# The second product of an attention score: from 64 partitions to all 128

## The chip, the cores and the metric

The kernel runs on one core of a Trainium2 chip. Its engines work side by side and each takes its own instructions in order: PE (TensorE) multiplies matrices, and its weight loads stand in the trace under their own name, PEld; DVE (VectorE), ACT (ScalarE) and POOL (GpSimd) work on elements; SP (SyncE) issues DMAs. On-chip data has 128 partitions; a matrix product sums over the partitions of its two operands. The metric is the device time of one execution in microseconds (us).

## The reference

Four transformer layers over 256 tokens and 1024 columns, batch 1: two layers of a first block (an attention of 16 heads with a mask of mixed dilations, and a differential attention of 16 score maps) and two of a second block (a gated delta rule, a windowed attention of 16 query heads on 2 key heads, and a feed-forward part). What matters here are the scores, which all three attentions compute in the same way:

```python
sc = jnp.einsum('mbqhd,mbkhd->mbhqk', qblk, ks,
                preferred_element_type=jnp.float32) * (dh ** -0.5)
...
sc = jnp.where(kpos[None, :] <= qpos[:, None], sc, NEG)
p = jax.nn.softmax(sc, axis=-1)
a = p[0] - lam * p[1]
return jnp.einsum('bhqk,bkhe->bqhe', a, vf)
```

These lines are the differential attention's; the other two differ in the mask, in what is made of the probabilities and in the number of keys. `dh` is 64. There are 96 score maps of 256 by 256 tokens: 16 + 16 in each of the two layers of the first block, and 16 in each of the two layers of the second. Above the diagonal block a map is masked, so that three of its four blocks of 128 by 128 are used.

## The kernel before

**Products in two parts.** TensorE reads its operands in a rounded format. So each f32 operand is split into a rounded part and what the rounding leaves out ("hi" and "lo"). A weight product is three matrix products into one PSUM bank: hi by hi, hi by lo, lo by hi (lines 312 to 314 for 512 columns a piece, lines 353 to 355 for 256).

**Scores.** A head has 64 columns, and two heads stand on the 128 partitions. `into_stack` (lines 454 to 463) writes a head's queries onto all 128: the rounded queries on one half of the partitions, their remainder on the other half. `into_keys` (lines 465 to 483) writes the rounded keys `kh` onto one half (line 474), and SP copies them to the other half by DMA (`twin`, line 480, two DMAs for a group of eight heads). So one product over 128 partitions gives (rounded + remainder of q) by rounded k (line 492). What the rounded keys leave out, `kl`, stands on a head's own half alone (line 475), and the second product (line 493) takes 64 partitions of the queries and of `kl`. A score map takes two such pairs, four products of 256 columns into one bank `sc`: tokens of block 1 first, then block 0.

**Order of the work.** The weight products are the main line. Everything else is queued by hand at a step of it (`at`, `tick`, with a lag in steps); the engines then run the instructions in the order in which the program wrote them. For one group of eight heads the order is: product for q, product for k, product for v, then the scores and the rest of each head between the weight products that follow. A head is: scores on PE, masked sum and row maximum on DVE (line 497), exponentials on ACT, in the first block a product with the mask's counts on DVE, transposes on PE (line 504), a copy on ACT (line 506), the product with v on PE (lines 510 to 512).

**Weights.** SP loads pieces of 256 rows (line 274, three buffers `raw`), ACT rounds them (line 284, `hi`), DVE subtracts (line 285, `lo`), with four buffers each of `hi` and `lo`.

**Second block.** Its windowed attention has two key heads. Their keys are written twice beside each other before the transpose, so that `kTh` and `kTl` (lines 958 and 959) stand on both halves already.

The tile `kl` is one of a ring of two buffers with the tag "Y"; a group of heads takes one of them.

Of the kernel before, what the change touches and what calls it, by code (L numbers as in the profile page):

```python
# [12 lines left out]
F32 = mybir.dt.float32  # L13
# [3 lines left out]
ALU = mybir.AluOpType  # L17
# [14 lines left out]
def _tables():  # L32
    """Masks, the identity and rotary tables: shapes alone decide them."""
    p = np.arange(128)[:, None]
    f = np.arange(128)[None, :]
    parts = {}
    parts["ident"] = (p == f).astype(np.float32)

    def band(count):
        return np.concatenate([count(128 + p, f), count(128 + p, 128 + f), count(p, f)], 1)  # L40

    def mix(t, s):
        d = t - s
        near = ((d >= 0) & (d <= 128)).astype(np.float32)
        return near + ((d >= 0) & (d % 4 == 0)) + ((d >= 0) & (d % 16 == 0))

    ca = band(mix).astype(np.float32)
    parts["ca"] = ca
    parts["ba"] = np.where(ca > 0, 0.0, NEG)
    parts["bb"] = np.where(band(lambda t, s: (s <= t)), 0.0, NEG)  # L50
    parts["bs"] = np.where(band(lambda t, s: (s <= t) & (t - s < 128)), 0.0, NEG)
    upper = (p <= f).astype(np.float32)
    one = np.ones((128, 128), np.float32)
    parts["mi"] = np.concatenate([upper, one], 1)
    parts["ng"] = np.where(parts["mi"] > 0, 0.0, NEG)
    parts["b16"] = p // 16 == f // 16
    parts["nb16"] = -parts["b16"].astype(np.float32)
    half = np.arange(0, 16, 2, dtype=np.float32)
    inv = (1.0 / np.power(np.float32(THETA), half / np.float32(16))).astype(np.float32)
    ang = (np.arange(256, dtype=np.float32)[:, None] * inv[None, :]).astype(np.float32)  # L60
    c, s = np.cos(ang), np.sin(ang)
    cc = np.concatenate([c, c], 1).reshape(2, 128, 16).transpose(1, 0, 2).reshape(128, 32)
    ss = np.concatenate([-s, s], 1).reshape(2, 128, 16).transpose(1, 0, 2).reshape(128, 32)
    parts["cc"], parts["ss"] = cc, ss
    f2 = np.power(np.float32(THETA), -np.arange(8, dtype=np.float32) * np.float32(0.125))
    parts["if"] = np.broadcast_to(f2.astype(np.float32)[None, :], (128, 8))
    where, col = {}, 0
    for k, v in parts.items():
        where[k] = (col, v.shape[1])
        col += v.shape[1]  # L70
    return np.ascontiguousarray(np.concatenate(list(parts.values()), 1).astype(np.float32)), where
# [6 lines left out]
def body(ctx: ExitStack, tc: tile.TileContext, I, out, upto=None):  # L78
# [60 lines left out]
    def column_load(name):  # L139
        """A vector of the model's width, its 128-element pieces in the columns of vT."""  # L140
        n, c = int(np.prod(I[name].shape)) // 128, vcol[name]
        row = half_tile("row")[0:n, 0:128]
        nc.scalar.dma_start(row, rows(I[name], 0, n))

        def compute():
            p = wk([128, 512])
            T.transpose(p[:, 0:n], row, ident[0:n, 0:n])
            V.tensor_copy(vT[:, c:c + n], p[:, 0:n])
        return compute
# [4 lines left out]
    def lam_load():  # L154
        """The first block's lambda of each layer."""
# [36 lines left out]
    def trig():  # L192
        """Rotary tables of the second block, from the positions."""
# [94 lines left out]
    def feed():  # L288
        """Loads and splits ahead as far as the buffers released before the last step allow."""
# [26 lines left out]
    def proj(lh, evac, sweep=False):  # L316
        """[tokens, columns] of lh @ the next weights, one bank per token block; evac(bank, block)."""
# [26 lines left out]
    def proj_w(lh, evac):  # L344
        """[columns, tokens] of 512 columns: two banks of two 128-column chunks; evac(bank, index)."""
# [21 lines left out]
    def to_lh(lh, src, c0, t, scale=None):  # L367
        """Transposes the 512 columns of src [128 tokens of block t, 512] into chunks c0.. of lh, split."""
# [33 lines left out]
    def into_silu(dst, hr, gain=None):  # L402
        """(tanh(z/2) + 1) * z', z' before its norm factor: hr * dst is silu (hr None: a half of it)."""
# [14 lines left out]
    def rope(x, h, cc, ss):  # L418
        """x [128, h * 64] of one token block: turns the first 16 of every 64 columns, in place."""
# [15 lines left out]
    def turned(r, tabs, then, lag):  # L435
        """Scales, turns and transposes 8 heads, two of them on the partitions; then(bank, columns, block)."""
# [17 lines left out]
    def into_stack(dst, r, tabs):  # L454
        """Eight heads of queries into dst [128, 8, 256]: a head's rounded columns on one half of the partitions,
        the one of its place in its pair, and what they leave out on the other."""
# [8 lines left out]
    def into_keys(st, r, tabs):  # L465
        """Eight heads of keys: rounded ones on both halves of the partitions, what they leave out on their own."""
        def then(p, cols, t):
            if t == 0:
                st["kh"] = act.tile([128, 8, 256], F32R, name="kh", tag="LT", bufs=1)
                st["kl"] = act.tile([128, 4, 256], F32R, name="kl", tag="Y", bufs=2)  # L470
            for i in range(2):
# [3 lines left out]
                V.tensor_tensor(out=st["kl"][a, :, cols], in0=p[a], in1=h.bitcast(F32), op=ALU.subtract)  # L475
            if t == 1:
                def twin():
                    for i in range(2):
                        a, b = halves(i)
                        nc.sync.dma_start(st["kh"][b, i:8:2, :].bitcast(F32), st["kh"][a, i:8:2, :].bitcast(F32))  # L480
                at(0, twin)
# [4 lines left out]
    def scores(q, kh, kl, i, bias):  # L486
        """Masked scores of one head, [t1 x s0 | t1 x s1 | t0 x s0], and their row maxima; i is its place in its pair."""
        sc = wk([128, 512], "sc")
        half = slice(64 * i, 64 * i + 64)
        for o, t in ((0, 1), (256, 0)):  # L490
            c = slice(128 * t, 128 * t + 128)
            T.matmul(sc[:, o:o + 256], q[:, c], kh, start=True, stop=False)
            T.matmul(sc[:, o:o + 256], q[half, c], kl[half], start=False, stop=True)  # L493
# [26 lines left out]
    def gate_first(gate):  # L520
        """gate <- (gate + 1) * bank"""
# [4 lines left out]
    def gate_second(gate, m1, lm, g):  # L526
        """m1 + (gate + 1) * bank, halved, transposed and split into lm"""
# [13 lines left out]
    def rstd_root(dst, a, b, c=0.0):  # L541
        """dst <- (a + b + c)^-1/2"""
# [3 lines left out]
    def rstd(dst, a, b):  # L546
        """dst * ROOT = rsqrt((a + b) / DM + eps)"""
        rstd_root(dst, a, b, DM * 1e-6)

    def prepare(t, scale, groups=(0, 1), lag=1.2):  # L550
        """Column groups of token block t of X are ready: their transposes for the next products, and the norm factors."""
# [18 lines left out]
    def normed(t, r, scale, k, folded=None):  # L570
        """Queues the transposes of X's token block t times r * ROOT, for the next products; folded stands
        for the block's second column group."""
# [45 lines left out]
    def layer1(l, last):  # L618
# [4 lines left out]
        def queue(pitch, stages, lead=4):  # L623
            """Queues one head's stages behind those of the heads before it."""
# [5 lines left out]
        def attend_a(q, k, v, sz, la, g):  # L630
            st = {}

            def s_(h):
                if h % 4 == 0:
                    st["den", h // 4] = tiny(8, "den")
                s, mx = scores(q[:, h, :], k["kh"][:, h, :], k["kl"][:, h // 2, :], h % 2, tb_("ba"))
# [49 lines left out]
        def attend_b(q, k, v, sz):  # L686
            st = {}

            def s_(h, m):
                if m == 0:  # L690
                    st["den", h] = tiny(4, "denb")
                s, mx = scores(q[:, 2 * h + m, :], k["kh"][:, 2 * h + m, :], k["kl"][:, h, :], m, tb_("bb"))
# [101 lines left out]
        def out_evac(g):  # L794
            def evac(acc, t):
# [16 lines left out]
                def both():  # L812
                    # r0 = rsqrt(m1 + eps), m1 and m2 the means of the squares before and after the product with fw:
                    # the two norms' factors are r0 and r0 * rsqrt(r0^2 m2 + eps) = rsqrt(m2 + eps * (m1 + eps))
# [35 lines left out]
    def post(accs, g, t, ss, gain, then, scale=None):  # L850
        """X[:, t] += rmsnorm(scale[0] * accs) * gain, scale[1] being ROOT times scale[0]; its two column banks coming one after the other."""
# [16 lines left out]
    def layer2(l, last):  # L868
# [3 lines left out]
        # small columns: beta, decay, keys and values of the windowed heads  # L872
# [23 lines left out]
        def small_rest():  # L896
            G.tensor_scalar(beta, beta, 0.5, 0.5, op0=ALU.mult, op1=ALU.add)
            G.tensor_scalar(nsink, sinks[:, 16 * l:16 * l + 16], -1.0, None, op0=ALU.mult)
            # softplus(x) = max(x, 0) + log1p(u), u = exp(-|x|), log1p(u) = 2 artanh(u / (2 + u))
# [31 lines left out]
        def sums():  # L931
            """Running sums of the log decays: heads on the partitions, by way of DRAM on all of them, and in columns."""
# [37 lines left out]
        def into_conv(m0, emit):  # L970
            """Causal convolution and silu of two chunks a bank, the taps shifting along the tokens."""
# [49 lines left out]
        def dn_rest(hh, dq, dk, pn, start):  # L1021
            """Queues the delta rule of 4 heads behind its q and k."""
# [64 lines left out]
            # Y = (I + LT)^-1 of the diagonal blocks, Xi its transpose: blocks of 16 by substitution,  # L1087
            # each with its rows on one partition, then by doubling
# [40 lines left out]
            def eights(rows):  # L1129
                """The two diagonal blocks of 8, row by row from the last; blk holds -LT."""  # L1130
# [9 lines left out]
            def corner(last):  # L1140
                """The block between them: inverse * (-LT) * inverse, its first product kept in blk's unused corner."""
# [28 lines left out]
            def level_y(lev, t):  # L1170
                # only these blocks count, and nothing that does comes from the others
# [20 lines left out]
            def outputs(t):  # L1192
# [16 lines left out]
                # f = s (mean(o^2) s^2 + eps)^-1/2, halved for the gate  # L1209
# [55 lines left out]
        def windowed(q, g, y):  # L1265
            st = {}

            def s_(h):
                if h % 4 == 0:
                    st["den", h // 4] = tiny(8, "den")  # L1270
                s, mx = scores(q[:, h, :], kTs[0][:, g, :], kTs[1][:, g, :], h % 2, tb_("bs"))
# [271 lines left out]
```

## Time and profile before

| what | value |
|---|---|
| time, median of 3 runs | 1807.46 us (1804.73 to 1810.01) |
| profiled execution, span from its first to its last instruction | 1810.5 us |
| PE busy | 1780.4 us, 98% |
| weight loads (PEld) busy | 1509.4 us, 83% |
| DVE busy | 1165.3 us, 64% |
| ACT busy | 1013.3 us, 56% |
| POOL busy | 323.9 us, 18% |

The page gives the profiled execution its span and no other time; the first of the three runs, at 1810.01 us, lies next to it. "Busy" counts any time in which an instruction of the engine is on its way. Matrix products overlap one another, and their ends are modelled, so a busy PE need not be a PE that works as fast as it can. The distance from the start of one product to the start of the next tells more than the busy time.

### The profile page before, as it was taken

What the parts mean: (1) busy time and instruction counts of PE and PEld (TensorE: products, weight loads), DVE (VectorE), ACT (ScalarE), POOL (GpSimd) and SP (SyncE); (2) the same over time, 40 slices, a digit from 0 to 9 for tenths busy, and PEclk for the clock granted to TensorE, in tenths of its full rate; (3) what the DMA queues carried; (4) which work ended last, traced back from release to release, by engine and by line L of the source; (5) the groups of instructions that cost most, each with busy time, mean ns of one, the idle gap of its engine ahead of it and who ended that gap; (6) DMA issues with size and microseconds to landing.
All of it is one profiled execution on the core that took longest, in us unless ns stands there. A gap on an engine that the chain in (4) does not pass through costs nothing.

```text
span 1810.5 us, 26858 instructions
## 1 busy us (share of the span) xinstructions
PE 1780.4 (98%) x9865; PEld 1509.4 (83%) x9865; DVE 1165.3 (64%) x2109; ACT 1013.3 (56%) x1834; POOL 323.9 (18%) x555
## 2 busy tenths in 40 slices
PE   8999999999999999999999999999999999999998
PEld 7788778887877788798888888998898888889997
DVE  5666676665666766778666567555779574676555
ACT  6655565465555654566556546444665565555443
POOL 2122221021222210144221001000342230000000
PEclk8999999999999999999999999999999999999999
DMA  6555455555444555564333455666554332555664
GB/s 199 176 146 150 141 155 160 173 178 173 140 133 138 160 165 171 158 184 134 105 83 88 152 175 178 193 187 187 154 161 134 90 92 82 185 172 178 186 186 140
DMA packets 157651, 278.06 MB, mean 154 GB/s; under 512 B 20304, under 2 KB 28240, under 8 KB 157520
## 3 DMA queue, kind: packets, MB, share of 16 engines
q1 hardware_dynamic: 156560, 273.64, 50.3%
q0 software_dynamic: 720, 2.62, 0.4%
q8 instruction: 78, 1.28, 0.3%
q14 instruction: 53, 0.43, 0.1%
q10 hardware_dynamic: 240, 0.09, 0.0%
HBM read 270.53 MB, written 1.59 MB: 150 GB/s over the span
## 4 chain that ended last, share of the span: by engine, by line
PE 46%; DVE 5%; DMA 3%; ACT 2%; POOL 1%; issue 1%; SPq 0%; DVEq 0%; POOLq 0%; ACTq 0%
PE acc L312 5%; PE acc L314 5%; PE acc L313 5%; PE acc L353 4%; PE acc L355 4%; PE acc L354 4%; PE facc L313 3%; PE facc L312 3%; PE facc L314 3%; DVE lo L285 2%; PE inv L1175 1%; PE inv L1165 1%; DMA raw<-in_w_in_dram 1%; PE sc L493 1%; ACT hi L284 1%
## 5 line engine op out<-in xcount | busy, mean ns | idle before, releaser
L285 DVE TENSOR_TENSOR lo<-raw,hi 128x1024 fp32r<-128x1024 f32 (+1 forms) x504 | 620.7, 1236 | 373.8 <-ACT hi L284 356.6
L284 ACT ACTIVATE hi<-raw 128x1024 fp32r<-128x1024 f32 (+1 forms) x504 | 527.8, 1052 | 357.7 <-PE acc L314 156.3
L312 PE MATMUL acc<-hi,lhi 128*128 128x512 f32 (+1 forms) x1344 | 559.6, 416 | 3.0 <-ACT lhi L385 3.0
L314 PE MATMUL acc<-hi,llo 128*128 128x512 f32 (+1 forms) x1344 | 528.3, 393 | 1.0 <-DVE llo L388 0.9
L313 PE MATMUL acc<-lo,lhi 128*128 128x512 f32 (+1 forms) x1344 | 526.6, 392 | 0.6 <-DVE lo L285 0.6
L314 PEld LDWEIGHTS acc<-hi,llo 128*128 128x128 f32 x1344 | 254.8, 190 | 57.8 <-DVE llo L388 3.8
L312 PEld LDWEIGHTS acc<-hi,lhi 128*128 128x128 f32 x1344 | 256.4, 191 | 50.1 <-ACT lhi L385 3.5
L313 PEld LDWEIGHTS acc<-lo,lhi 128*128 128x128 f32 x1344 | 256.6, 191 | 41.7 <-DVE lo L285 2.4
L353 PE MATMUL acc<-lhi,hi 128*128 128x256 f32 x832 | 240.5, 289 | 0.0
L355 PE MATMUL acc<-lhi,lo 128*128 128x256 f32 x832 | 236.1, 284 | 0.0
L354 PE MATMUL acc<-llo,hi 128*128 128x256 f32 x832 | 236.1, 284 | 0.0
L353 PEld LDWEIGHTS acc<-lhi,hi 128*128 128x128 f32 x832 | 159.9, 192 | 2.2 <-issue 0.6
L354 PEld LDWEIGHTS acc<-llo,hi 128*128 128x128 f32 x832 | 160.2, 193 | 0.7
L355 PEld LDWEIGHTS acc<-lhi,lo 128*128 128x128 f32 x832 | 160.0, 192 | 0.0
L506 ACT ACTIVATE ptS<-pt 128x384 f32<-128x384 f32 x80 | 39.2, 490 | 109.8 <-PE pt L504 109.5
L312 PE MATMUL facc<-hi,fh 128*128 128x512 f32 x256 | 99.9, 390 | 0.0
L313 PE MATMUL facc<-lo,fh 128*128 128x512 f32 x256 | 99.9, 390 | 0.0
L314 PE MATMUL facc<-hi,fl 128*128 128x512 f32 x256 | 99.7, 390 | 0.0
L543 POOL TENSOR_SCALAR pf<-pss 128x1 f32<-128x1 f32 x8 | 3.7, 457 | 468.2 <-ACT pj L853 468.2
L497 DVE CUSTOM_DVE_ANT_0 s<-sc,tab 128x256 f32<-128x256 f32 x192 | 60.5, 352 | 20.9 <-PE sc L493 19.9
L314 PEld LDWEIGHTS facc<-hi,fl 128*128 128x128 f32 x256 | 48.1, 188 | 10.0
L312 PEld LDWEIGHTS facc<-hi,fh 128*128 128x128 f32 x256 | 48.2, 188 | 9.6
(309 smaller groups left out, 2330.9 us busy)
## 6 DMA issues: line engine op xcount, KB each, us to landing
raw<-in_w_in_dram SPq DMA_DIRECT2D x272, 512.0 KB, 3.7
raw<-in_w_ff_dram SPq DMA_DIRECT2D x128, 512.0 KB, 4.4
raw<-in_w_proj_a_dram SPq DMA_DIRECT2D x16, 512.0 KB, 3.7
raw<-in_w_proj_b_dram SPq DMA_DIRECT2D x16, 512.0 KB, 3.6
raw<-in_w_out_dram SPq DMA_DIRECT2D x16, 512.0 KB, 3.9
raw<-in_w_up_sw_dram SPq DMA_DIRECT2D x16, 512.0 KB, 3.7
raw<-in_w_up_dn_dram SPq DMA_DIRECT2D x16, 512.0 KB, 3.7
raw<-in_w_o_dram SPq DMA_DIRECT2D x16, 512.0 KB, 3.7
```

The source lines that it names most:

```text
L284: S.activation(hi[:, :, :o], raw[:, :, :o], AF.Copy)
L285: V.tensor_tensor(out=lo[:, :, :o], in0=raw[:, :, :o], in1=hi[:, :, :o].bitcast(F32), op=ALU.subtract)
L312: T.matmul(a, lh[0][:, c, sl], hi[:, cc, :n], start=first, stop=False)
L313: T.matmul(a, lh[0][:, c, sl], lo[:, cc, :n], start=False, stop=False)
L314: T.matmul(a, lh[1][:, c, sl], hi[:, cc, :n], start=False, stop=last)
L353: T.matmul(a, hi[:, c % 2, sl], lh[0][:, c, :], start=(c == 0 and m % 2 == 0), stop=False)
L354: T.matmul(a, hi[:, c % 2, sl], lh[1][:, c, :], start=False, stop=False)
L355: T.matmul(a, lo[:, c % 2, sl], lh[0][:, c, :], start=False, stop=(c == 7 and m % 2 == 1))
L493: T.matmul(sc[:, o:o + 256], q[half, c], kl[half], start=False, stop=True)
L497: V.tensor_tensor_reduce(s[:, a:b], sc[:, a:b], bias[:, a:b], 1.0, FMIN, ALU.add, ALU.max, accum_out=mx[:, j:j + 1])
L506: S.activation(r, pt, AF.Copy)
L1165: T.matmul(p[:, i, :], LT[:, i, DG[t]:DG[t] + 128], st["Xi"][:, t, i, :], start=True, stop=True)
```

## The change

What the rounded keys leave out is written into two tiles in place of one, one for the even and one for the odd heads of the pairs, and SP copies each to the other half of the partitions with a DMA of its own. The second product then takes all 128 partitions: the same queries as the first one, by `kl`. It adds the remainder of the queries by the remainder of the keys, which the kernel before left out. The windowed attention passes `kTl` as it is, with all its partitions. The change also drops comments and docstrings, which moves no instruction; line numbers grow by 3 from `twin` on.

```diff
     def into_keys(st, r, tabs):
         def then(p, cols, t):
             if t == 0:
                 st["kh"] = act.tile([128, 8, 256], F32R, name="kh", tag="LT", bufs=1)
-                st["kl"] = act.tile([128, 4, 256], F32R, name="kl", tag="Y", bufs=2)
+                st["kl"] = [act.tile([128, 4, 256], F32R, name="kl", tag="Y", bufs=2) for _ in range(2)]
             for i in range(2):
                 a, _ = halves(i)
                 h = st["kh"][a, i:8:2, cols]
                 S.activation(h, p[a], AF.Copy)
-                V.tensor_tensor(out=st["kl"][a, :, cols], in0=p[a], in1=h.bitcast(F32), op=ALU.subtract)
+                V.tensor_tensor(out=st["kl"][i][a, :, cols], in0=p[a], in1=h.bitcast(F32), op=ALU.subtract)
             if t == 1:
                 def twin():
                     for i in range(2):
                         a, b = halves(i)
                         nc.sync.dma_start(st["kh"][b, i:8:2, :].bitcast(F32), st["kh"][a, i:8:2, :].bitcast(F32))
+                    for i in range(2):
+                        a, b = halves(i)
+                        nc.sync.dma_start(st["kl"][i][b].bitcast(F32), st["kl"][i][a].bitcast(F32))
                 at(0, twin)
         return turned(r, tabs, then, 5.3)[1]
...
-    def scores(q, kh, kl, i, bias):
+    def scores(q, kh, kl, bias):
         sc = wk([128, 512], "sc")
-        half = slice(64 * i, 64 * i + 64)
         for o, t in ((0, 1), (256, 0)):
             c = slice(128 * t, 128 * t + 128)
             T.matmul(sc[:, o:o + 256], q[:, c], kh, start=True, stop=False)
-            T.matmul(sc[:, o:o + 256], q[half, c], kl[half], start=False, stop=True)
+            T.matmul(sc[:, o:o + 256], q[:, c], kl, start=False, stop=True)
...
-                s, mx = scores(q[:, h, :], k["kh"][:, h, :], k["kl"][:, h // 2, :], h % 2, tb_("ba"))
+                s, mx = scores(q[:, h, :], k["kh"][:, h, :], k["kl"][h % 2][:, h // 2, :], tb_("ba"))
...
-                s, mx = scores(q[:, 2 * h + m, :], k["kh"][:, 2 * h + m, :], k["kl"][:, h, :], m, tb_("bb"))
+                s, mx = scores(q[:, 2 * h + m, :], k["kh"][:, 2 * h + m, :], k["kl"][m][:, h, :], tb_("bb"))
...
-                s, mx = scores(q[:, h, :], kTs[0][:, g, :], kTs[1][:, g, :], h % 2, tb_("bs"))
+                s, mx = scores(q[:, h, :], kTs[0][:, g, :], kTs[1][:, g, :], tb_("bs"))
```

On SP, where the first group of heads writes its keys, the queue of DMAs reads as follows (- before, + after; `raw` is a piece of weights; the brackets name the semaphores that an instruction waits for):

```order
 L480 DMA kh<-kh 64x4x256 [waits DMAHW4_49,Activation_49]
 L480 DMA kh<-kh 64x4x256 [waits Activation_49]
-L274 DMA raw<-in_w_in_dram 128x2x512 [waits DMAHW1_49,DVE_49]
+L483 DMA kl<-kl 64x1024 [waits DVE_49] x2
+L274 DMA raw<-in_w_in_dram 128x2x512 [waits DMAHW1_49,DMAHW0_49,DVE_49]
```

Two DMAs of 64 partitions by 4 KB go in between the copies of `kh` and the next load of weights, and they wait for DVE. From the second group on the second of them waits for PE as well, since the buffer had a tenant before.

On PE the order is the same before and after. Where the first group's first score stands, before:

```order
L314 MATMUL acc<-hi,llo 128x512
L492 MATMUL sc<-kh,qk 128x256 [waits DMAHW4_49,DVE_49,Activation_49]
L493 MATMUL sc<-kl,qk 128x256 [waits DVE_49]
L492 MATMUL sc<-kh,qk 128x256
L493 MATMUL sc<-kl,qk 128x256
L312 MATMUL acc<-hi,lhi 128x512
```

And after:

```order
L314 MATMUL acc<-hi,llo 128x512
L495 MATMUL sc<-kh,qk 128x256 [waits DMAHW4_49,DVE_49,Activation_49]
L496 MATMUL sc<-kl,qk 128x256 [waits DMAHW6_49,DVE_49]
L495 MATMUL sc<-kh,qk 128x256
L496 MATMUL sc<-kl,qk 128x256
L312 MATMUL acc<-hi,lhi 128x512
```

Nothing moved; the first product with `kl` of a group now waits for a DMA too (the rows give the output's shape, not the 64 or 128 partitions that are summed).

## Rows read from the trace of the kernel before

**Rows 1.** The page: span, and busy time of each engine.
```profile
span 1810.5 us, 26858 instructions
PE 1780.4 (98%) x9865; PEld 1509.4 (83%) x9865; DVE 1165.3 (64%) x2109; ACT 1013.3 (56%) x1834; POOL 323.9 (18%) x555
```

**Rows 2.** What PE waited for, longest first: total us, times, longest us.
```profile
PE pn L1014 <- ACT hcv L1016: 5.9, 6, 1.5
```

**Rows 3.** Timeline of PE, one score: start us, us, instruction, partitions*columns.
```profile
120.90 0.28 PE L492 MATMUL sc<-kh,qk 128*128 128x256 f32 x1
121.11 0.38 PE L493 MATMUL sc<-kl,qk 64*128 64x256 f32 x1
121.42 0.38 PE L492 MATMUL sc<-kh,qk 128*128 128x256 f32 x1
121.73 0.38 PE L493 MATMUL sc<-kl,qk 64*128 64x256 f32 x1
122.05 0.50 PE L312 MATMUL acc<-hi,lhi 128*128 128x512 f32 x1
122.38 0.40 PE L313 MATMUL acc<-lo,lhi 128*128 128x512 f32 x1
122.61 0.39 PE L314 MATMUL acc<-hi,llo 128*128 128x512 f32 x1
```

**Rows 4.** Timeline of the weight loads in the same score.
```profile
120.68 0.19 PEld L492 LDWEIGHTS sc<-kh,qk 128*128 128x128 f32 x1
121.11 0.18 PEld L493 LDWEIGHTS sc<-kl,qk 64*128 64x128 f32 x1 [0.24 <-issue]
121.42 0.19 PEld L492 LDWEIGHTS sc<-kh,qk 128*128 128x128 f32 x1
```

**Rows 5.** All products of line 493: count, ns min/median/max, first and last start.
```profile
L493 PE MATMUL sc<-kl,qk x128: 378/382/383, 58.0 to 656.5; 64*128 64x256 f32 x128
L493 PE MATMUL sc<-kTl,qk x64: 378/381/384, 889.3 to 1523.0; 64*128 64x256 f32 x64
```

**Rows 6.** Timeline of PE, weight products of 256 columns.
```profile
941.51 0.28 PE L354 MATMUL acc<-llo,hi 128*128 128x256 f32 x1
941.63 0.28 PE L355 MATMUL acc<-lhi,lo 128*128 128x256 f32 x1
941.75 0.28 PE L353 MATMUL acc<-lhi,hi 128*128 128x256 f32 x1
```

**Rows 7.** First and last group: SP, DVE, and PE's first product with `kl`.
```profile
52.20 2.05 SPq L480 DMA_DIRECT2D kh<-kh  x2
53.66 0.69 DVE L475 TENSOR_TENSOR kl<-tp,kh 64x512 fp32r<-64x512 f32 x1 [0.66 <-ACT kh L474]
56.00 0.38 SPq L274 DMA_DIRECT2D raw<-in_w_in_dram  x1
57.99 0.38 PE L493 MATMUL sc<-kl,qk 64*128 64x256 f32 x1
...
601.91 1.94 SPq L480 DMA_DIRECT2D kh<-kh  x2
605.60 0.37 SPq L274 DMA_DIRECT2D raw<-in_w_in_dram  x1
608.17 0.38 PE L493 MATMUL sc<-kl,qk 64*128 64x256 f32 x1
```

**Rows 8.** DMA issues of 50:58, then 600:608: count, KB, median us to landing.
```profile
kh<-kh SPq DMA_DIRECT2D x2, 256.0 KB, 4.4
...
kh<-kh SPq DMA_DIRECT2D x2, 256.0 KB, 3.1
```

**Rows 9.** A windowed head's exponentials on ACT, and its transposes on PE.
```profile
946.29 0.19 ACT L1282 ACTIVATION_READ_ACCUMULATOR e<-s,nm 128x1 f32 x1
946.92 0.27 PE L504 MATMUL pt<-ident,e 128*128 128x128 f32 x1
```

**Rows 10.** Eight heads of the first block: us, then busy us by engine, clock.
```profile
57.50:107.00 49.50, 49.50 (x238) 38.55 (x238) 31.84 (x83) 28.08 (x47) 11.97 (x26) 1.00 0.50 150
```

## The prediction

> **What bounds the kernel now.** I read the page first: PE is busy for 1780.4 us of a span of 1810.5 us, no other engine for more than two thirds of it [rows 1]. PE's waits come next. The longest item among them adds up to 5.9 us over the whole run [rows 2]. So PE nearly always has something to do, and the time is the sum of the distances between its instructions: whatever makes one of these shorter shortens the kernel, as long as the other engines keep up.
>
> Busy time doesn't show whether a product is dear, since products overlap. So I read the timeline of PE around a score, by starts [rows 3]. Four products of 256 columns start at 120.90, 121.11, 121.42 and 121.73 us, and the weight product behind them at 122.05: distances of 0.21, 0.31, 0.31 and 0.32 us. The weight product itself takes 0.33 us until the next one starts, and that one 0.23 us, though both have 512 columns. Beside it, weight products of 256 columns start every 0.12 us [rows 6], with new weights each time. A score product is no larger; it takes more than twice as long.
>
> The weight loads show why [rows 4]. The load of the first score product starts at 120.68 us, 0.22 us ahead of its product, so it is hidden behind the product before. That of the second (64 partitions) starts at 121.11 us, at the same time as its own product, and PEld had been idle for 0.24 us. The third (128 partitions again) starts at 121.42 us, once more with its product. Each change between 128 and 64 partitions thus takes away the overlap: the load of the next product doesn't start until the one before is through. A score has four such changes, the fourth into the weight product that follows. That one product is not an odd case: the 192 products of line 493 take 378 to 384 ns with medians of 382 and 381 [rows 5].
>
> The Trainium skill says the same of a change of the array's mode (TensorEngine Tiling (Array Packing), Key Properties): it drains TensorE. By that rule all four go; the page has no price for one.
>
> **What the change saves.** After the change all products of a score sum over 128 partitions, like those of the main line, with the same columns and formats. The trace has no score product behind another of 128 partitions. The bounds for its distance are 0.12 us, as weight products of this shape [rows 6], and 0.31 us, if nothing changes [rows 3]. I take 0.12: partitions, columns and number format are the same, each of those products has its own load as well, and they too add to one bank one after the other. From the first score product to the second product behind the score it was 122.38 - 120.90 = 1.48 us. It becomes 4 x 0.12 + 0.23 = 0.71 us. That is 0.77 us for a score and 96 x 0.77 = 74 us for the kernel. If what follows the score had no part in it (the 0.10 us between 0.33 and 0.23), it would be 96 x 0.67 = 64 us. Most scores are followed by a product of the main line, as here, so I take 73.
>
> **What it adds.** Sixteen DMAs of 256 KB, two for each of eight groups. They cost nothing on PE if they land before the first product with `kl`. In the first group SP has issued both copies of `kh` at 52.20 + 2.05 = 54.25 us, and DVE's last `kl` is ready at 53.66 + 0.69 = 54.35 us. That one is for the odd heads; the even heads' copy can be issued at 54.25. The nearest rows for landing are the copies of `kh`, which have the same size: 4.4 us in that group, 3.1 us in the last [rows 8]. So it lands at 57.4 to 58.7 us. The first product with `kl` started at 57.99 us [rows 7] and would now start at about 57.9, with 0.12 us in place of 0.21 behind the first: a wait of 0 to 0.8 us, once; I take 0.4. In the last group it is 601.91 + 1.94 = 603.85 us, landing at 607.0 (or 608.3 at the slow rate), for a product that starts at 608.17 less 0.09: hidden, or 0.2 us late. Should the same happen in all eight groups at the worst value, it is 6 us.
>
> Behind these DMAs on SP stands the next load of weights. An issue takes about 0.6 us (the last pair of `kh` 1.94 us with a wait for ACT in between), so SP is free again at about 54.25 + 1.2 = 55.5 us and 603.85 + 1.2 = 605.1 us. The next load went out at 56.00 and 605.60 us [rows 7]: it isn't held up. That cover is 0.5 us; without it the load is later by as much, in front of three buffers of raw pieces and four of split ones. I put it at nothing. The writes of DVE and ACT are the same in number and size. The second ring buffer that a group takes is written only after the transposes of its keys on PE, which stand behind all scores of the group before, so it waits for nothing that `kh` doesn't wait for already.
>
> **What is late next.** The rest of a head takes as long as before, while PE arrives sooner. Between a head's score and its transposes PE has one score of another head, so the transposes come up to 0.77 us earlier against the exponentials, and 0.10 us for the product behind its own score. Among the tightest is a windowed head whose exponentials end at 946.29 + 0.19 = 946.48 us for transposes at 946.92 [rows 9]: 0.44 us to spare, so 0.87 - 0.44 = 0.43 us of waiting. If all 96 were like it: 41 us; at none of them: 0. DVE, the busiest beside PE in eight heads of the first block, works 31.84 of 49.50 us [rows 10]. With 8 x 0.77 = 6 us less that is 31.84 of 43.3, or 74%, and ACT 28.08 of 43.3, or 65%. Neither becomes the bound. I take 4 us, some ten heads like that one.
>
> **Sum.** 73 - 0.4 - 4 = 69 us off the profiled span of 1810.5 us: 1741.5. That execution lies 3.0 us over the median of the runs, 1807.46 us, and I take the same 69 us off that: 1738.5, near 1738 us. The clock is granted in full in these stretches (1.00) [rows 10], and I expect it to stay so.
>
> **Rivals.**
>
> *The waits take a third or more.* Same saving on PE, but DVE's and ACT's queues, in which a head's work stands behind splits of weights, answer too late in most heads. For it: the head at 946 us. Against it: the spare time of 26% on DVE, and waits of PE that are next to nothing now [rows 2]. With 25 to 41 us given back the time is 1759 to 1775 us, most likely near 1762.
>
> *Partitions don't matter.* A product over 64 partitions would cost what one over 128 does, and the slow distance would come from something that stays, such as two products adding to one bank in turn, or the weights of queries. Then it stays at 0.31 us, and the time at 1807 us, within 3 us. Against it: the weight products add to one bank too, at 0.12 us [rows 6], and the weight product behind a score is slowed as well [rows 3]. What speaks for it is that a load of 64 partitions takes 0.18 us and one of 128 takes 0.19 [rows 4]: the work itself is no smaller.
>
> This is also what the Trainium skill has (TensorE: Matmul & The Clock Gate, LDWEIGHTS): a weight load goes by columns, not by the contraction. Taken alone, the page's rule would leave the time where it is; the trace agrees on the load, and shows the change of size as a cost beside it.
>
> *Slower: copies of `kl` that come late.* The first product with `kl` of every group holds PE until its copy has landed. To pass 1807 by 0.3% (5 us), the eight groups must lose 73 + 5 = 78 us, 9.8 us each. Its place is line 496 behind SP's line 483. In the first group the copy has 57.9 - 54.25 = 3.6 us until it is missed, in the last 4.2, so it decides from a landing of some 13.5 us on. The rows show 3.1 and 4.4 us [rows 8].
>
> **How the numbers follow.** Within 0.3% is about what a measurement of this kernel can't tell from no change: 1802 to 1813 us. The forecast gets 0.81, at 1731 to 1750 us: the full 74 us with no waits gives 1733.5, the runs scatter by some 2.6 us, and 6 us for late copies with 8 for waits and 2 for runs on the other side give about 1750. Waits that take a third get 0.13, late copies 0.02, no effect 0.04. To hold the time 8 times in 10 the range goes from 1731 up to 1755, a part of the way into the first rival. Faster is 0.94, no difference 0.04, slower 0.02.
>
> **What would show it.** In the profile after: line 496 with 128*128 in place of 64*128, its weight load starting ahead of its product; starts of 0.12 us inside a score, and 0.23 us for the weight product behind; PE's busy time down by about 70 us; a wait of PE for a copy of `kl` below 1 us in the first group and none later; waits of transposes (line 507) of some 4 us in all. I am wrong if starts of 0.2 us or more stay between the two products of a score, if the waits of PE grow past 20 us, or if the time that goes lies outside the 96 scores.

## The result and the profile after

The changed kernel takes 1748.9 us in the median (1747.13 to 1749.48, 4 runs) against 1808.32 us (1804.73 to 1810.01, 4 runs): a ratio of 0.9671, 95% interval 0.9656 to 0.9686. It is faster, and the time lies inside the range given. The forecast was 1738 us, 69 us off; 59 us came. What follows asks whether the reason was the right one, and where the other 10 us went.

The page of the changed kernel, its span and the busy time of each engine (before: [rows 1]):

```profile
span 1745.2 us, 26891 instructions
...
PE 1709.6 (98%) x9865; PEld 1485.3 (85%) x9865; DVE 1162.5 (67%) x2109; ACT 1013.2 (58%) x1834; POOL 329.2 (19%) x555
```

PE's busy time fell by 70.8 us, that of DVE and ACT hardly moved, and PE is still busy for 98% of the span. The number of products is the same.

The timeline of PE in the changed kernel, at three places: the first score of the first group, a head's transposes, and the score that [rows 3] show of before:

```profile
57.24 0.28 PE L495 MATMUL sc<-kh,qk 128*128 128x256 f32 x1
59.02 0.36 PE L496 MATMUL sc<-kl,qk 128*128 128x256 f32 x1 [1.50 <-DMA kl<-kl]
...
101.57 0.39 PE L515 MATMUL o<-v,ptS 128*128 128x64 f32 x2
102.67 0.79 PE L507 MATMUL pt<-ident,pc 128*128 128x128 f32 x3 [0.72 <-DVE pc L655]
...
117.54 0.28 PE L495 MATMUL sc<-kh,qk 128*128 128x256 f32 x1
117.66 0.28 PE L496 MATMUL sc<-kl,qk 128*128 128x256 f32 x1
117.78 0.28 PE L495 MATMUL sc<-kh,qk 128*128 128x256 f32 x1
117.90 0.28 PE L496 MATMUL sc<-kl,qk 128*128 128x256 f32 x1
118.02 0.40 PE L312 MATMUL acc<-hi,lhi 128*128 128x512 f32 x1
118.25 0.40 PE L313 MATMUL acc<-lo,lhi 128*128 128x512 f32 x1
```

Read the starts in the last part: four products 0.12 us apart and the weight product behind them 0.23 us, 0.71 us in all where it was 1.48 us. The weight loads of the same score, also of the changed kernel (before: [rows 4]):

```profile
117.32 0.19 PEld L495 LDWEIGHTS sc<-kh,qk 128*128 128x128 f32 x1
117.55 0.19 PEld L496 LDWEIGHTS sc<-kl,qk 128*128 128x128 f32 x1
117.66 0.19 PEld L495 LDWEIGHTS sc<-kh,qk 128*128 128x128 f32 x1
```

The load of line 496 starts at 117.55 us, 0.11 us ahead of its product at 117.66; before, both started together. A load still takes 0.19 us, but it lies under the product before it.

All products of line 496 in the changed kernel (before: [rows 5]): count, ns min/median/max, first and last start:

```profile
L496 PE MATMUL sc<-kl,qk x128: 278/283/358, 59.0 to 618.4; 128*128 128x256 f32 x128
...
L496 PE MATMUL sc<-kTl,qk x64: 274/282/287, 847.0 to 1458.1; 128*128 128x256 f32 x64
```

Medians of 382 and 381 ns became 283 and 282. What PE waited for in the changed kernel (total us, times, longest), two rows that the list of before doesn't have at this size:

```profile
PE pt L507 <- DVE pc L655: 3.0, 4, 0.8
PE sc L496 <- DMA kl<-kl: 3.0, 3, 1.5
```

### The profile page after: what moved, and what is told of

It reads as the page before. It is cut to its first block, busy times and chain, and to the rows that moved or that the text cites. A ratio compares the mean times of both kernels' runs of the same rounds, so it can differ in the third digit from the quotient of the medians.

```text
span 1745.2 us, 26891 instructions
## 1 busy us (share of the span) xinstructions
PE 1709.6 (98%) x9865; PEld 1485.3 (85%) x9865; DVE 1162.5 (67%) x2109; ACT 1013.2 (58%) x1834; POOL 329.2 (19%) x555
## 4 chain that ended last, share of the span: by engine, by line
PE 48%; DVE 6%; ACT 2%; DMA 1%; issue 1%; POOL 0%; DVEq 0%; POOLq 0%; SPq 0%; ACTq 0%
PE acc L314 6%; PE acc L312 6%; PE acc L313 6%; PE acc L353 4%; PE acc L354 4%; PE acc L355 4%; PE facc L313 3%; PE facc L312 3%; PE facc L314 3%; DVE lo L285 2%; PE inv L1178 1%; PE inv L1168 1%; PE tp L371 1%; ACT hi L284 1%; PE pt L507 1%
## 5 line engine op out<-in xcount | busy, mean ns | idle before, releaser
L312 PE MATMUL acc<-hi,lhi 128*128 128x512 f32 (+1 forms) x1344 | 551.2, 410 | 2.5 <-ACT lhi L385 2.5
```

Source lines behind the costliest of these rows:

```text
L312: T.matmul(a, lh[0][:, c, sl], hi[:, cc, :n], start=first, stop=False)
```

## The experiments

**Where the 64 partitions stand in the order.** The kernel before, with its four products sorted:

```diff
-        for o, t in ((0, 1), (256, 0)):
-            c = slice(128 * t, 128 * t + 128)
-            T.matmul(sc[:, o:o + 256], q[:, c], kh, start=True, stop=False)
-            T.matmul(sc[:, o:o + 256], q[half, c], kl[half], start=False, stop=True)
+        for part in range(2):
+            for o, t in ((0, 1), (256, 0)):
+                c = slice(128 * t, 128 * t + 128)
+                if part == 0:
+                    T.matmul(sc[:, o:o + 256], q[:, c], kh, start=o == 0, stop=False)
+                else:
+                    T.matmul(sc[:, o:o + 256], q[half, c], kl[half], start=False, stop=o == 256)
```

> The kernel before, with the four products of a score in another order: both products with the rounded keys first (128 partitions), then both with their remainder (64). Same products, same operands, no copies of kl. The theory that the change between 128 and 64 partitions is what costs: two changes a score in place of four. Distances by start of 0.12 (128 behind 128), 0.21 (64 behind 128), some 0.20 (64 behind 64, a load still exposed, nothing to drain) and 0.21 us, then 0.33 us for the weight product behind: 1.07 in place of 1.48 us, so 0.4 us x 96 = 38 us off, about 1770 us. Rival, a product over 64 partitions is slow by itself wherever it stands: its 0.31 us stay, and the time stays within 3 us of 1808.

Measured: 1771.79 us (1770.63 to 1771.95), ratio 0.9798 (0.9784 to 0.9813), against 1807.07 us: 35 us less with the same products and the same operands. The timeline of PE in this kernel (the two products of a line are merged, with their count):

```profile
117.65 0.40 PE L494 MATMUL sc<-kh,qk 128*128 128x256 f32 x2
117.97 0.50 PE L496 MATMUL sc<-kl,qk 64*128 64x256 f32 x2
118.40 0.50 PE L312 MATMUL acc<-hi,lhi 128*128 128x512 f32 x1
118.74 0.40 PE L313 MATMUL acc<-lo,lhi 128*128 128x512 f32 x1
```

From the first score product to the second weight product it is 118.74 - 117.65 = 1.09 us, expected 1.07. So a product over 64 partitions isn't always dear; what it stands behind decides.

**All four on 64 partitions.** The kernel before, with the first product of each pair on 64 partitions too (it leaves out the remainder of the queries by the rounded keys):

```diff
-            T.matmul(sc[:, o:o + 256], q[:, c], kh, start=True, stop=False)
+            T.matmul(sc[:, o:o + 256], q[half, c], kh[half], start=True, stop=False)
```

> The kernel before with all four products of a score on the 64 partitions of the head's own half (it leaves out the remainder of the queries by the rounded keys). In the kernel with the sorted order the second of two products over 64 partitions came 0.22 us behind the first, and this tells why. Theory that only the change of size costs: inside a score there is none, so that from the second on the products stand 0.12 us apart; one change on the way in and one on the way out. By start: 0.10 more before the first, then 0.22, 0.12, 0.12, 0.21, 0.33 us: 1.10 in place of 1.48 us, 0.38 us x 96 = 36 us off, about 1771 us. Rival, products over 64 partitions of one half never overlap their own weight load, change or not: 0.22 us each, 1.30 us, 17 us off, about 1790 us.

Measured: 1770.72 us (1768.77 to 1771.89), ratio 0.9801 (0.9787 to 0.9814), against 1805.87 us: 35 us less. PE's timeline in this kernel, and the weight loads of the first two score products:

```profile
118.37 0.39 PE L314 MATMUL acc<-hi,llo 128*128 128x512 f32 x1
118.69 0.38 PE L492 MATMUL sc<-kh,qk 64*128 64x256 f32 x1
118.91 0.28 PE L493 MATMUL sc<-kl,qk 64*128 64x256 f32 x1
119.03 0.28 PE L492 MATMUL sc<-kh,qk 64*128 64x256 f32 x1
119.14 0.28 PE L493 MATMUL sc<-kl,qk 64*128 64x256 f32 x1
119.35 0.50 PE L312 MATMUL acc<-hi,lhi 128*128 128x512 f32 x1
119.68 0.40 PE L313 MATMUL acc<-lo,lhi 128*128 128x512 f32 x1
...
118.68 0.18 PEld L492 LDWEIGHTS sc<-kh,qk 64*128 64x128 f32 x1 [0.35 <-issue]
118.79 0.19 PEld L493 LDWEIGHTS sc<-kl,qk 64*128 64x128 f32 x1
```

The second to fourth product over 64 partitions start 0.22, 0.12 and 0.11 us after the one before; over all 96 scores of this kernel the medians are 0.22, 0.12 and 0.12 us. Behind one of their own size they are as quick as those over 128. The first behind a change has its load exposed: the load starts at 118.68 us, with its product at 118.69, while that of the second starts 0.12 us ahead of its own at 118.91. The first weight product behind the score pays too, with 0.21 us until it starts and 0.33 us until the next one does. This settles it between the two theories: the change of size costs, at both ends, not the size. It also puts a reason right: the 0.22 us between the two products over 64 partitions in the sorted order are those of a first product behind a change, and not of a second load that is still exposed, as that expectation had it; its 0.20 us came near by luck.

**The second block alone.** `scores` takes all 128 partitions for the windowed heads, 64 for the others; no copy is added.

```diff
-    def scores(q, kh, kl, i, bias):
+    def scores(q, kh, kl, i, bias, whole=False):
...
-        half = slice(64 * i, 64 * i + 64)
+        half = slice(None) if whole else slice(64 * i, 64 * i + 64)
...
-                s, mx = scores(q[:, h, :], kTs[0][:, g, :], kTs[1][:, g, :], h % 2, tb_("bs"))
+                s, mx = scores(q[:, h, :], kTs[0][:, g, :], kTs[1][:, g, :], h % 2, tb_("bs"), True)
```

> The kernel before, with the second product over 128 partitions in the second block's windowed attention alone (its keys stand on both halves already; adds remainder by remainder there). No copy is added. Theory of the change of size: 32 scores x 0.77 = 24.6 us less what the waits there take, and since the profile after shows 26.6 us gained in the second block (65.2 in all, 38.6 at its start): 1782 to 1785 us. Rival, the gain is one of the whole pipeline (the copies, the tiles or the order of the queues of the first block): clearly less than 20 us.

Measured: 1787.66 us (1785.38 to 1790.45), ratio 0.9893 (0.9874 to 0.9911), against 1807.07 us: 19.4 us less, beside 24.6 us for 32 scores, and 3 to 6 us short of the expectation. By the time alone the case stays open, as the rival had "clearly less than 20 us"; the starts decide. The two lots of products of line 493 stand side by side in its profile:

```profile
L493 PE MATMUL sc<-kl,qk x128: 378/381/383, 55.3 to 653.9; 64*128 64x256 f32 x128
...
L493 PE MATMUL sc<-kTl,qk x64: 278/283/287, 884.8 to 1496.5; 128*128 128x256 f32 x64
```

Laid side by side with the copies-alone kernel (next) by the starts of PE's products, the windowed scores are 24.4 us shorter and the others the same: the saving came in full where the edit was made and nowhere else. The spans of the two profiles differ by 21.7 us, so that 2.7 us are lost outside the scores. The expectation rested on 26.6 us read against the profiled execution of before, which was too much: see the base of the sum below.

**The copies alone.** The changed kernel with its two tiles and its sixteen DMAs, the second product on 64 partitions (the calls pass the head's place in its pair again).

```diff
+        half = slice(64 * i, 64 * i + 64)
...
-            T.matmul(sc[:, o:o + 256], q[:, c], kl, start=False, stop=True)
+            T.matmul(sc[:, o:o + 256], q[half, c], kl[half], start=False, stop=True)
```

> The changed kernel with its two kl tiles and its copies, but the second product takes 64 partitions as before; the copies are made and read by nobody. Theory that the copies cost only where PE waits for them: the time of the kernel before, within 2 us (1806 to 1810). Rival, the copies cost by themselves (they hold up SP or the loads of weights behind them): 3 to 10 us slower than before.

Measured: 1807.81 us (1806.97 to 1809.85), ratio 1.0003 (0.9994 to 1.0012). Within that interval (1 us less to 2 us more) the copies cost nothing by themselves: whatever they do to SP and to the loads of weights behind them doesn't show in the time. Its DMA issues over the whole run (count, KB, median us to landing):

```profile
kh<-kh SPq DMA_DIRECT2D x16, 256.0 KB, 3.3
kl<-kl SPq DMA_DIRECT2D x16, 256.0 KB, 4.4
```

**Zeros in place of copies.** The other half of each `kl` tile set to zero by POOL for every group, and no copies of `kl`:

```diff
+                for i in range(2):
+                    G.memset(st["kl"][i][halves(i)[1]].bitcast(F32), 0.0)
...
-                    for i in range(2):
-                        a, b = halves(i)
-                        nc.sync.dma_start(st["kl"][i][b].bitcast(F32), st["kl"][i][a].bitcast(F32))
```

> The changed kernel, but the other half of each kl tile is set to zero by POOL in place of the DMA's copy, so that the remainder of the queries by the remainder of the keys is left out, as in the kernel before. The second product still sums over 128 partitions. Theory that the copies land late: PE's waits for kl (3.0 us in the profile after, 1.5 of it in the first group) go, and nothing else changes: 3 us less than the changed kernel, 1746 us. Rival, the late part is the whole group's chain on DVE and ACT and not the copy: the wait moves to another releaser, and the time is that of the changed kernel, 1749 us.

Measured: 1747.04 us (1746.61 to 1747.76), ratio 0.9663 (0.9649 to 0.9678). The time lies between the two expectations, and its interval overlaps that of the changed kernel, so it decides nothing. The wait for `kl` is gone; waits for POOL's `tok` and ACT's `hcv` are longer by 1.2 and 3.0 us.

**Zeros once.** The two tiles taken and zeroed at the start and kept through the first block, and no copies of `kl`:

```diff
-                st["kl"] = [act.tile([128, 4, 256], F32R, name="kl", tag="Y", bufs=2) for _ in range(2)]
+                st["kl"] = kz
...
-                    for i in range(2):
-                        a, b = halves(i)
-                        nc.sync.dma_start(st["kl"][i][b].bitcast(F32), st["kl"][i][a].bitcast(F32))
...
+    kz = []
...
+    for i in range(2):
+        kz.append(act.tile([128, 4, 256], F32R, name="kl", tag="Y", bufs=2))
+        G.memset(kz[i][halves(i)[1]].bitcast(F32), 0.0)
```

> The changed kernel with the other halves of the two kl tiles set to zero once at the start, and the tiles kept through the first block; no copies and no work on POOL per group (remainder by remainder is left out in the first block, as before). With zeros per group PE's wait for POOL's tok grew from 2.5 to 3.7 us. Theory that the zeroing on POOL cost that: PE's waits for kl (3.0 us) go and nothing comes, 3 us less than the changed kernel, 1745 to 1746 us. Rival, the waits for POOL and ACT are scatter: as with zeros per group, 1747 us.

Measured: 1743.77 us (1743.05 to 1746.08), ratio 0.9657 (0.9644 to 0.9670). That is 5 us below the changed kernel by medians and 2.5 us by ratios (0.0014 of 1808), so in the direction of the first theory; the intervals overlap, and the runs' times don't show it. The two profiles are clearer: laid side by side by starts, the products of the first block's scores stand 4.0 us closer in all, 3.5 us of it ahead of the three products that had waited for `kl`, and everything else sums to 0.1 us.

**Later transposes.** The changed kernel, and the one with zeros set once, with three lags longer: that of the transposes of the mixed-dilation heads, and those of the transposes and of the products with v of the windowed heads:

```diff
-                            ((-0.6, s_), (0.9, e_), (1.1, c_), (3.5, t_), (9.8, v_))])
+                            ((-0.6, s_), (0.9, e_), (1.1, c_), (4.1, t_), (9.8, v_))])
...
-                at(k + 2.8, lambda h=h: t_(h))
-                at(k + 3.7, lambda h=h: v_(h))
+                at(k + 3.2, lambda h=h: t_(h))
+                at(k + 4.1, lambda h=h: v_(h))
```

> The changed kernel with the transposes of the mixed-dilation heads queued 0.6 steps later and transposes and products with v of the windowed heads 0.4 steps later. Laid side by side instruction by instruction with the copies-alone kernel, the changed kernel loses some 7 us between the products and the transposes of probabilities, more than the 3.0 us that its list of waits gives for them. Theory that the transposes now come too early: 4 to 7 us less than the changed kernel, 1742 to 1745 us. Rival, DVE and ACT hold PE back wherever it is: the waits move to the next hand-over, and the time stays within 2 us of 1749.

> The zeros set once and the later transposes together. If the two losses are apart from each other they add: 7 to 10 us less than the changed kernel, 1739 to 1742 us. If they are one and the same (a group that starts late hands over late), no more than the better of the two.

Measured: 1751.26 us (1748.24 to 1757.62), ratio 0.9699 (0.9678 to 0.9720), and 1747.25 us (1745.73 to 1748.77), ratio 0.9672 (0.9659 to 0.9685). Neither gained: the first expectation failed by 6 us and more, its rival (within 2 us of 1749) by a little, and the two edits together are 3.5 us above the zeros alone, with intervals that overlap. PE's waits in the kernel with both edits:

```profile
PE o L510 <- ACT ptS L506: 4.3, 2, 2.1
...
PE pt L504 <- DVE pc L653: 1.2, 4, 0.3
```

The wait of the transposes shrank from 2.9 us (with zeros alone) to 1.2, and a new one of 4.3 us came, of the products with v for the copy of the transposed probabilities on ACT, one a layer in the second block. The wait moved one step down the head, as the rival had it for the windowed heads.

**Later in the first block alone.** The zeros once, and only the first of the three lags:

```diff
-                            ((-0.6, s_), (0.9, e_), (1.1, c_), (3.5, t_), (9.8, v_))])
+                            ((-0.6, s_), (0.9, e_), (1.1, c_), (4.1, t_), (9.8, v_))])
```

> The zeros set once, and only the first block's transposes of mixed-dilation heads 0.6 steps later; the windowed heads stay where the changed kernel has them. Both together (windowed ones later too) gave 1747.25 us, against 1743.77 without either; laid side by side, the first block came out 1.4 us ahead and the second 3.8 us behind, with a new wait of PE for the copies of transposed probabilities (4.3 us) in the second. Theory that these are two separate places: 1.4 us less than the zeros alone, 1742 us. Rival, what is gained in the first block is given back where its hands meet the second: 1744 us or more.

Measured: 1743.05 us (1740.67 to 1745.69), ratio 0.9640 (0.9627 to 0.9653). Its median is the lowest of all. By ratio it is 5.6 us (0.0031 of 1808) below the changed kernel, with intervals that just don't meet; beside the zeros alone it is less than the scatter, and the spans of the two profiled executions are the same, 1741.2 us. The wait of 4.3 us for ACT's copies doesn't stand in its profile, so that loss came from the lags of the windowed heads. The 1.4 us of the first block are not shown: the transposes wait 1.6 us less than with the zeros alone (1.3 us in place of 2.9), but waits for POOL's `tok` and ACT's `hcv` are longer by 1.3 and 1.7 us.

**Copies in turn.** The changed kernel, each `kl` copy right behind the `kh` copy of its heads:

```diff
                         nc.sync.dma_start(st["kh"][b, i:8:2, :].bitcast(F32), st["kh"][a, i:8:2, :].bitcast(F32))
-                    for i in range(2):
-                        a, b = halves(i)
                         nc.sync.dma_start(st["kl"][i][b].bitcast(F32), st["kl"][i][a].bitcast(F32))
```

> The changed kernel with the four copies of a group issued in turn: rounded keys of the even heads, their remainder, rounded keys of the odd heads, their remainder. The first score of a group needs the first two. Theory that PE waits for the queue of copies in front: the even heads' kl goes out some 0.7 us earlier, PE's waits for kl go from 3.0 us to 1.5 us or less, and the time falls by 1 to 2 us, to 1747 to 1748 us. Rival, the copy is slow by itself (4.3 us from issue to landing against 3.3 us of kh): the order doesn't matter, 1749 us and waits of 3 us.

Measured: 1749.57 us (1748.78 to 1750.38), ratio 0.9675 (0.9662 to 0.9688). PE's waits in this kernel:

```profile
PE pt L505 <- DVE pc L653: 3.6, 5, 0.8
...
PE pt L505 <- DVE llo L378: 0.8, 1, 0.8
PE pt L505 <- DVE pc L714: 0.7, 2, 0.5
...
PE sc L494 <- DMA kl<-kl: 0.5, 1, 0.5
```

The wait for `kl` went from 3.0 to 0.5 us as the first theory had it, and the time didn't: waits of the transposes grew by 2.1 us (0.6, 0.8 and 0.7). Neither theory was right as it stood. The rival's "slow by itself" isn't the whole of it: the copies of `kh`, half of which are third in this order, land in 4.5 us in the median, where the copies-alone kernel had 3.3; those of `kl` take 4.8 in place of 4.4.

## Why the prediction was right

**The mechanism.** It is shown, by three runs beside the change itself. Sorting the products, with nothing else altered, gave 35 of some 38 us; putting all of them on 64 partitions gave 35 of 36 us; the edit in the second block alone shortened its scores and no others. The distances by start came out within 0.03 us of what was expected, one by one. The rival that partitions don't matter falls: a load over 64 partitions does take as long as one over 128, but between the sizes the overlap is lost. The rival with late copies falls by the changed kernel's own waits: 3.2 us for copies in all, where it needed 78, and the longest recorded landing of a copy of `kl` was 5.5 us, where it needed some 13.5. (The copies alone, at 1.0003, show that they cost nothing elsewhere; there no product waits for them.)

One reading of the prediction was too strong: that behind a change a load doesn't start until the product before is through. By [rows 3] and [rows 4] the load at 121.11 us starts 0.07 us ahead of that product's modelled end (120.90 + 0.28 us). What the rows show is that it starts with its own product and not ahead of it. Why the engine doesn't begin it earlier isn't shown.

**The sum.** PE executes the same 9865 recorded products in the same order in the copies-alone kernel and in the changed one. So their distances by start can be laid side by side, and the differences add up to that of the spans, 1805.1 - 1745.2 = 59.9 us:

| distances by start | forecast, us | measured, us |
|---|---|---|
| between the products of a score | | 45.14 |
| from a score to the next product | | 18.29 |
| from that to the one behind it | | 9.21 |
| *scores in all* | 73 | 72.64 |
| waits for copies of `kl` | -0.4 | -3.18 |
| into the transposes of probabilities | -4 | -7.55 |
| all the rest | 0 | -2.06 |
| *sum* | 69 | 59.85 |

The term that carries the forecast was right within half a microsecond. The step of a product over 128 partitions that the trace before didn't show, bounded by 0.12 and 0.31 us, came out at 0.12.

**The terms that were mis-sized** are the two that were to be "late next".

*Copies.* I took 0 to 0.8 us in the first group and at most 0.2 in the last, and named as a sign a wait below 1 us in the first group and none later. Measured were 3.18 us by the starts: PE was idle for 1.50 us in the first group, until 59.02 us, and for 0.73 us in each of two others. The price of a landing was the one that failed: I took that of the copies of `kh` without company. The DMA issues of 50 to 60 us in the changed kernel:

```profile
kh<-kh SPq DMA_DIRECT2D x2, 256.0 KB, 4.6
kl<-kl SPq DMA_DIRECT2D x2, 256.0 KB, 5.3
```

With four copies under way at once the later two took 5.3 us here and 4.4 us in the median of the copies-alone run, beside 4.6 and 3.3 us for the earlier two; before, with two alone, it was 4.4 us in the first group and 3.1 in the last [rows 8]. The bound of 6 us for all eight groups held.

*Transposes.* I took 4 us, some ten heads like the windowed one at 946 us, which waits for its exponentials on ACT; it is 7.55 us. That head lost 0.16 us, and all windowed heads together 1.57 us. The greater part lies where I hadn't looked: 4.62 us in four heads of the first block, one in each group of mixed-dilation heads, at 1.1 to 1.2 us each, and they are held by DVE. The list of waits gives 3.0 us for these, since it counts the time in which PE stands idle after the modelled end of a product. From 101.57 us, the start of the two products ahead, to 102.67 us, the start of the transposes, it is 1.10 us, 0.72 of which the profile calls a wait. What held them, on ACT and DVE in the changed kernel:

```profile
98.33 0.79 ACT L648 ACTIVATE e<-s,nm 128x256 f32<-128x256 f32 x2
...
99.38 0.69 DVE L676 TENSOR_TENSOR yo<-o,rdh 128x512 f32<-128x512 f32 x1 [2.32 <-POOL rdh L674]
99.99 1.22 DVE L285 TENSOR_TENSOR lo<-raw,hi 128x1024 fp32r<-128x1024 f32 x1
101.12 1.49 DVE L655 SCALAR_TENSOR_TENSOR pc<-e,tab 128x256 f32<-128x256 f32 x1
102.54 0.08 DVE L655 DVE_READ_ACCUMULATOR pc<-e,tab 128x1 f32 x1
```

The same place in the copies-alone kernel, on PE and DVE:

```profile
103.97 0.39 PE L516 MATMUL o<-v,ptS 128*128 128x64 f32 x2
104.19 0.50 PE L508 MATMUL pt<-ident,pc 128*128 128x128 f32 x3
...
102.82 0.08 DVE L656 DVE_READ_ACCUMULATOR pc<-e,tab 128x1 f32 x1
```

The head's exponentials were ready at 99.12 us. But in DVE's queue a split of weights of 1.22 us stands ahead of its product with the mask's counts, ahead of that an instruction for which DVE stood idle for 2.32 us, waiting for POOL, and the transposes start 0.05 us after the product's sum is read. DVE isn't busy all the time; it takes its work in an order that fitted PE's old pace. Here is the step of the term that failed: I let PE come at most 0.87 us earlier against the rest of a head, as if the other engines kept up from head to head. At this head PE came 2.40 us earlier than in the copies-alone kernel (101.57 in place of 103.97) and DVE 0.28 us (102.54 in place of 102.82): 2.12 us, against a spare time of 1.29 us there (102.90 to 104.19). What PE gains on single heads adds up: it was 0.88 and 1.63 us at the transposes of the two heads before. The instruction of POOL that DVE waits for comes 0.26 us earlier (98.75 in place of 99.01); what holds it was not followed further.

This is the first rival's mechanism at a smaller size: 7.55 of the 72.6 us, 10%, and with the copies and the rest 12.8 us, 18%, where a third was its least.

**The base of the sum.** The profiled execution of before had a span of 1810.5 us, that of the copies-alone kernel 1805.1, with the same work on PE. Against the first the changed kernel's profile shows 65.3 us, 5.4 more than like for like; none of these 5.4 us lies in the scores. The medians of the runs (59.4 us) agree with the second. I took the offset from the median of the runs as constant, and it wasn't.

**The numbers.** 1748.9 us lies in the upper half of 1731 to 1755; the case forecast (1731 to 1750) holds it.

**What stays open.** Which of the small waits a change of the queue takes away for good. The runs with later transposes and with copies in turn each shortened the wait they aimed at and brought others of much the same size. Of the 10 us given back, the zeros once with the first block's transposes later regain some 4 (by the spans of the profiles) to 6 us (by the runs). Whether DVE's order could be written anew for the rest wasn't tried.

## What to carry to other kernels

A matrix product that sums over half the partitions between others that sum over all of them pays twice for the change, and the busy time doesn't show it. Look at the starts, and at whether a weight load begins ahead of its product or with it. Filling the other half (with zeros, if there is nothing to add) gave 59 to 62 of 72.6 us back here, and sorting the products by size 35. When the bound engine gets faster, price the hand-overs to it by their spare time head by head, not from the list of waits, and set against it all that the engine has gained by then, not the gain of one head.

## What the runs showed of the hardware

- Products of 256 columns over 64 partitions of one half, behind one another, start 0.12 us apart (all four on 64 partitions), as those over 128 do (the changed kernel). The first behind a change has its load exposed: 0.22 us until the next one starts for 256 columns over 64 partitions behind 128, and 0.33 us in place of 0.23 for 512 columns over 128 behind 64.
- From a product over 128 partitions to one over 64 with 256 columns it is 0.21 us [rows 3] in place of 0.12; when both ends of a product are a change, it is 0.31 us.
- Copies of 256 KB from one half of the partitions to the other, four in a row (the copies-alone kernel): the first two land in 3.3 us in the median, the two behind them in 4.4 us; in the first group the latter took 5.9 us there and 5.3 us in the changed kernel.
